# Transformer block on one core: the order of products, weight loads and stores in the feed-forward part

## Chip, core and metric

The kernel runs on one core of a Trainium2 chip, in one launch. The metric is device time in microseconds. TensorE is PE in the profile, VectorE DVE, ScalarE ACT, GpSimd POOL; SyncE (SP) issues nearly all the DMAs.

## What is computed

One layer for 2048 tokens of width 1024: a combined input projection, two kinds of attention, an output projection with residual, and a SwiGLU feed-forward part of width 2816. The change touches the last lines:

```python
h = h + jnp.einsum('bse,ed->bsd', mix, w_out[l])
u2 = rms_norm(h, norm2_w[l])
gate = jnp.einsum('bsd,df->bsf', u2, w_gate[l])
up = jnp.einsum('bsd,df->bsf', u2, w_up[l])
h = h + jnp.einsum('bsf,fd->bsd', jax.nn.silu(gate) * up, w_down[l])
```

## The kernel before

The feed-forward part runs over `steps`: two halves of 1024 tokens, and in each half 11 groups of 256 hidden columns. A step does `gate`, sometimes `down`, then `up`. Each matrix is cut into 2 x 2 blocks, and the 8 block products are replaced by 7 (combinations of blocks are formed first, and the results are added up in three running sums). Every number is kept as two f16 parts, high and low, so a block product is 12 matmuls of 512 columns (three part pairs by four slices of 128 rows), and `gate` or `up` is 7 products, 84 matmuls. `down` is 84 matmuls for each step whose activations it takes up, two steps at a time, so 168 in every second step.

`quad` writes the seven products in this order: `pa` (first part), two `pm`, `pa` again (accumulated on its first part), `pd`, `pm`, `pd` again. ACT copies `pa` at L1014 before it is accumulated on, and DVE reads `pd` at L1031 before its second part; L1035 and L1038 add the last two. `on_gate` applies silu on ACT (L1049), `on_up` multiplies on DVE (L1069) and forms the combinations of the activations.

The weights come in the first half through `load_ffn`, once for each of gate, up and down ("g", "u", "d") and step. A load takes one of two staging buffers (`stages`, filled by a DMA at L909 or L911), squares it on ACT into `sq`, of which there is one buffer (L937 for g and u, L189 for d), gets column maxima through PE into a PSUM tile `fsc` (8 matmuls at L945 for g and u, two small ones at L182 for d), makes a power-of-two scale in a chain of one-column DVE instructions (L175 to L204), and splits the blocks into high (ACT, L215) and low parts (DVE, L220). Four combinations are formed with `tt` on POOL (L98); three of them overwrite blocks of `stages`, one goes to `sx`. At the end the split weights are stored to `split` (L986), and the second half reads them back (L928).

`begin` runs a load up to the squares; `end` runs the rest. Both are called from hooks inside `gate`, `up` and `down`: the square of the next gate weights stands in the middle of `gate`, the rest of it at the start of `down`, and so on. In `up`, the down weights are ended and then the next up weights begun. `build_x` makes the last four token tiles of the second half's input in the background of the first two steps; `tick` advances it.

The program order is not the order on an engine: the framework places each instruction with a timeline of its own, and once placed, an engine takes its instructions strictly in that order. `tc.issue_after(x)` puts an edge into that plan: what is inside is placed behind x. PSUM has 8 tiles, taken in turn by `pst`.

Of the kernel before, what the change touches and what calls it, by code (L numbers as in the profile page):

```python
# [40 lines left out]
CU = 3  # L41
# [18 lines left out]
def block(tc, a, out):  # L60
# [3 lines left out]
    with top:  # L64
# [113 lines left out]

        def across(dst, pt, cols):
            k = len(cols)  # L180
            for j, c in enumerate(cols):
                PE.matmul(pt[:, P * j : P * j + P], lhsT=c.to_broadcast([P, P]), rhs=id32[:], start=True, stop=True)  # L182
            DVE.tensor_reduce(dst, pt[:, : P * k], op=ALU.max, axis=AX.X)
# [689 lines left out]
        with ExitStack() as ph2:  # L873
# [32 lines left out]

            def fetch(st, f0, nme):
# [12 lines left out]
            def load_ffn(half, fg, names, W):  # L920
                eng = "ADP" if fg == 0 else WE
                sc = scales.setdefault(fg, {})
                for nme in names:
                    if half == 1:
                        yield
                        late = nme == "d" and fg == NFG - 1
                        w16 = (fd if nme == "d" and not late else fw).tile([P, 7, 2, 512], F16, tag="wd" if nme == "d" and not late else "wgu", bufs=2, name=nm("w" + nme))
                        SP.dma_start(w16[:].rearrange("p o s n -> p (o s n)"), split[fg, "gud".index(nme)])  # L928
                        W[nme] = w16
                        continue  # L930
# [12 lines left out]
                    def columns(m):  # L943
                        for k in range(KT):
                            PE.matmul(pt[:, :256], lhsT=ones[:], rhs=sq[:, 256 * k : 256 * k + 256], start=k == 0, stop=k == KT - 1)  # L945
                        DVE.tensor_reduce(m, pt[:, :256], op=ALU.max, axis=AX.X)

                    scale_end((lambda m: across(m, pt, cols)) if nme == "d" else columns, r[:], p[:], True, sW)
                    sc[nme] = (r, p, sW)
                    sW = sc[nme][2]  # L950
                    tte = "DP" if fg == 0 else "P"
                    sx = fw.tile([P, 512], F32, tag="sx", bufs=1, name=nm("sx"))

                    def put(o, src, n):
                        split_weight(w16[:, o : o + n, 0], w16[:, o : o + n, 1], src, 512 * n, sW, eng)

                    if nme == "d":
                        sv = st.rearrange("p (f h n) -> p h f n", f=2, h=2)
                        b11, b21, b12, b22 = sv[:, 0, 0], sv[:, 0, 1], sv[:, 1, 0], sv[:, 1, 1]
                        put(0, sv[:, 0], 2)  # L960
                        tt(sx[:], b22, b12, ALU.subtract, 512, tte)
                        tt(b12, b12, b11, ALU.subtract, 512, tte)
                        tt(b11, b22, b12, ALU.subtract, 512, tte)
                        tt(b21, b21, b11, ALU.subtract, 512, tte)
                        put(2, sv[:, 1], 2)
                        put(4, sv[:, 0], 2)
                        put(6, sx[:].unsqueeze(1), 1)
                    else:
                        sv = st.rearrange("p (d k f n) -> p d k f n", d=2, k=4, f=2)
                        xv = sx[:].rearrange("p (k n) -> p k n", k=4)  # L970
                        wv = w16[:].rearrange("p o s (k n) -> p o s k n", k=4)

# [7 lines left out]
                        tt(blk(0, 0), blk(1, 0), blk(0, 0), ALU.subtract, 512, tte)  # L980
                        tt(blk(0, 1), blk(0, 1), blk(0, 0), ALU.subtract, 512, tte)
                        putk(2, sv[:, :, :, 1, :], 2)
                        putk(4, sv[:, :, :, 0, :], 2)
                        putk(6, xv.unsqueeze(1), 1)
                    W[nme] = w16
                    SP.dma_start(split[fg, "gud".index(nme)], w16[:].rearrange("p o s n -> p (o s n)"))  # L986
                if half == 0 and "g" in names:
# [12 lines left out]
            def product(ps_, wv, wo, X, xo, start, stop):  # L1000
                q = 0
                for kt in range(4):
                    for xi, wi in ((0, 0), (1, 0), (0, 1)):
                        PE.matmul(ps_[:].rearrange("p (t n) -> p t n", n=P), lhsT=wv[:, wo, wi, 128 * kt : 128 * kt + 128], rhs=X[xo][:, :, xi, kt, :], start=start and q == 0, stop=stop and q == 11, skip_group_check=not start)  # L1004
                        q += 1

            def quad(wv, X, tag, bufs, c11, hook=None):
                def cst():
# [7 lines left out]
                product(p6, wv, 4, X, 4, True, True)  # L1016
                DVE.tensor_tensor(u2[:], p6[:], u2[:], ALU.add)
                p7 = pst("pm")
# [12 lines left out]
                DVE.tensor_tensor(c22[:], pd[:], u3[:], ALU.add)  # L1031
                c11(1, 1, c22)
                p4 = pst("pm")
                product(p4, wv, 3, X, 6, True, True)
                DVE.tensor_tensor(u3[:], u3[:], p4[:], ALU.subtract)  # L1035
                c11(1, 0, u3)
                product(pd, wv, 5, X, 3, False, True)
                DVE.tensor_tensor(u2[:], u2[:], pd[:], ALU.add)  # L1038
                c11(0, 1, u2)

            def gate(W, X, hook=None):
                sg = {}
# [8 lines left out]

                quad(W["g"], X, "cg", 5, on_gate, hook)
                note("A", 2000)
                return sg

            def up(W, X, sg, hook=None, final=False):
                if final:
# [25 lines left out]

                quad(W["u"], X, "cu", CU, on_up, hook)
                note("D", 2440)
                return act

            def load_hs(half, j, final=False):
                if half == 1 and j % 2 and not final:
                    h = [stages[:, j // 2, D * q : D * q + D] for q in range(2)]  # L1090
# [6 lines left out]
            def down(half, units, hs, last, hook=None):  # L1097
# [3 lines left out]
                def prod(po, ao, wo, j, start=True):  # L1101
                    for u, (W, act) in enumerate(units):
                        for q, (xi, wi) in enumerate(((0, 0), (0, 1), (1, 0))):
                            PE.matmul(po[:], lhsT=act[:, ao, xi, 128 * j : 128 * j + 128], rhs=W["d"][:, wo, wi, :], start=start and u == 0 and q == 0, stop=u == nu - 1 and q == 2, skip_group_check=not start)  # L1104

# [12 lines left out]
                for j in range(4):  # L1118
                    if j == 2 and hook is not None:
                        hook()  # L1120
                    if j + 1 < 4:
                        hs.append(load_hs(half, j + 1, nu == 3))
                    h0, h1 = hs[j]
# [31 lines left out]
            def build_x():  # L1155
# [11 lines left out]
                for j in (2, 3):  # L1167
# [6 lines left out]
                    for z in (xa, xb):  # L1174
                        for h in range(2):
                            tr = pst("xtr")
                            for k in range(4):
                                PE.transpose(tr[:, P * k : P * k + P], z[:, 512 * h + P * k : 512 * h + P * k + P], id32[:])
                            ACT.copy(z[:, 512 * h : 512 * h + 512], tr[:])
# [40 lines left out]
            for i, (half, fg) in enumerate(steps):  # L1220
# [47 lines left out]
                if i == 0:  # L1268
                    tick(1)
                units.append((W, act))  # L1270
# [27 lines left out]
```

## Time and profile before

| | us |
|---|---|
| median of 3 runs (2700.67 to 2704.35) | 2701.52 |
| profiled execution, its own time | 2702.93 |
| its span | 2701.0 |
| feed-forward, first product starts at | 1425.19 |
| last `up` of the first half starts at | 2059.52 |

All stretches are in microseconds from the start of the span. A row of the timeline gives start, duration, engine, line, operation, tiles and how many were merged; in square brackets the idle time of the engine ahead of it and what ended that. Consecutive matmuls overlap, so the time that a product takes is read from start to start.

### The profile page before, as it was taken

How to read it: one execution, taken by the hardware profiler on the slowest of the kernel's cores; microseconds unless marked ns; L12 is line 12 of the kernel's file. 1: busy time of each engine (PE TensorE's matmuls, PEld its weight loads, DVE VectorE, ACT ScalarE, POOL GpSimd, SP SyncE). 2: the span in 40 equal slices, each digit the busy share in tenths (PEclk: the TensorE clock that was granted, in tenths of full speed). 3: DMA queues.
4: the chain of work that ended last, by engine and by line, in shares of the span. 5: the costliest groups of instructions: out<-in, count | busy, mean ns of one | idle time of the engine just before them, and what ended most of it. 6: DMA issues, size and time to landing. Idle time of an engine off the chain costs nothing. (4 is left out here: it accounts for less than half of the span.)

```text
span 2701.0 us, 50505 instructions
## 1 busy us (share of the span) xinstructions
PE 2508.6 (93%) x19628; PEld 1507.6 (56%) x19628; DVE 1959.8 (73%) x3712; ACT 1344.7 (50%) x2487; POOL 1517.8 (56%) x1097
## 2 busy tenths in 40 slices
PE   7998989899988989889999999999999999999999
PEld 4655656577776776567774444444444444444444
DVE  6898879899989889887866877778685543433434
ACT  4665656567978878765634534435352112111121
POOL 2578767768767767545665755665564332322323
PEclk9999999999999999999999999999999999999999
DMA  6778697768989989997996566565748744635532
GB/s 221 211 163 184 143 200 172 172 145 183 195 175 185 178 166 206 208 205 203 230 317 232 211 232 219 207 239 183 253 171 330 304 159 157 234 132 184 202 110 94
DMA packets 619584, 534.40 MB, mean 198 GB/s; under 512 B 480640, under 2 KB 548224, under 8 KB 609104
## 3 DMA queue, kind: packets, MB, share of 16 engines
q1 hardware_dynamic: 617520, 529.09, 70.1%
q8 instruction: 154, 2.52, 0.4%
q0 software_dynamic: 512, 1.36, 0.2%
q14 instruction: 86, 0.70, 0.1%
q10 hardware_dynamic: 1312, 0.72, 0.1%
HBM read 261.08 MB, written 147.32 MB: 151 GB/s over the span
## 5 line engine op out<-in xcount | busy, mean ns | idle before, releaser
L98 POOL TENSOR_TENSOR s<-z,s 128x1024 f16<-128x1024 f32 (+7 forms) x288 | 471.5, 1646 | 141.8 <-ACT s L89 118.2
L506 PE MATMUL sc<-kT,qT 128*128 128x512 f16 (+3 forms) x1520 | 382.7, 354 | 51.1 <-DVE z L622 18.6
L1104 PE MATMUL pd<-wd,act 128*128 128x512 f16 x1764 | 392.8, 380 | 5.3 <-DVE cu L1038 4.7
L621 DVE TENSOR_TENSOR_SCAN z<-z,sc 128x512 f32<-128x512 f32 (+3 forms) x320 | 352.8, 1112 | 56.5 <-ACT sc L619 34.6
L325 PE MATMUL pj<-w,xt 128*128 128x384 f16 x1920 | 354.6, 333 | 17.1 <-ACT raw L374 5.8
L1004 PEld LDWEIGHTS <-wu 128*128 128x128 f16 x1848 | 181.9, 98 | 224.6 <-issue 12.8
L1004 PEld LDWEIGHTS <-wg 128*128 128x128 f16 x1848 | 181.3, 98 | 222.9 <-issue 9.3
L517 PE MATMUL yp<-v,aT 128*128 128x64 f16 (+1 forms) x4896 | 271.2, 205 | 36.9 <-DMA aT<-s 35.7
L517 PEld LDWEIGHTS <-aT 128*128 128x128 f16 x4896 | 239.1, 100 | 114.4 <-DMA aT<-s 46.7
L98 POOL TENSOR_TENSOR act<-cg,act 128x512 f16<-128x512 f32 x109 | 150.7, 1393 | 259.4 <-ACT act L1063 259.4
L1104 PEld LDWEIGHTS <-act 128*128 128x128 f16 x1764 | 172.9, 98 | 213.5 <-issue 7.2
L325 PEld LDWEIGHTS <-xt 128*128 128x128 f16 x1920 | 187.8, 99 | 147.2 <-issue 23.4
L89 ACT CAST s<-z 128x128 f16<-128x128 f32 (+7 forms) x215 | 173.3, 810 | 135.9 <-DMA aT<-s 44.6
L98 POOL TENSOR_TENSOR stages<-stages 128x512 f32<-128x512 f32 x97 | 171.4, 1767 | 116.5 <-DVE wg L220 42.2
L618 ACT ACTIVATE z<-sc,c 128x512 f32<-128x512 f32 (+3 forms) x320 | 211.2, 665 | 24.4 <-PE sc L506 12.4
L98 POOL TENSOR_TENSOR hs<-hs,cu 128x512 f32<-128x512 f32 x102 | 133.6, 1317 | 159.3 <-DVE hs L1110 59.7
L506 PEld LDWEIGHTS <-qT 128*128 128x128 f16 x1520 | 128.8, 99 | 119.7 <-issue 23.9
L831 PE MATMUL po<-wo,mt 128*128 128x256 f16 x1536 | 182.4, 279 | 12.6 <-DVE xf L834 8.6
L1063 ACT CAST act<-cg 128x512 f16<-128x512 f32 x126 | 76.7, 616 | 231.1 <-DVE cg L1069 192.7
L1110 DVE SCALAR_TENSOR_TENSOR hs<-pd,c,hs 128x512 f32<-128x512 f32 x144 | 106.0, 747 | 115.0 <-PE pd L1104 105.3
L341 PE MATMUL pj<-xt,w 128*128 128x128 f16 x2304 | 177.4, 222 | 6.2 <-DVE v L363 5.2
L1004 PE MATMUL pm<-X,wu 128*128 128x512 f16 x792 | 179.8, 381 | 2.1 <-ACT cg L1049 1.7
(254 smaller groups left out, 4812.3 us busy)
## 6 DMA issues: line engine op xcount, KB each, us to landing
xt<-xs SPq DMA_DIRECT2D x112, 512.0 KB, 4.5
hs<-hd SPq DMA_DIRECT2D x72, 512.0 KB, 4.5
hd<-hs SPq DMA_DIRECT2D x56, 512.0 KB, 5.9
split<-wg SPq DMA_DIRECT2D x11, 1792.0 KB, 6.9
split<-wu SPq DMA_DIRECT2D x11, 1792.0 KB, 6.7
split<-wd SPq DMA_DIRECT2D x11, 1792.0 KB, 6.8
wg<-split SPq DMA_DIRECT2D x11, 1792.0 KB, 7.5
wd<-split SPq DMA_DIRECT2D x11, 1792.0 KB, 9.0
```

What stands on the lines that cost most here:

```text
L89: ACT.copy(dst, src)
L98: (DVE if e == "D" else POOL).tensor_tensor(dst, a_, b_, op)
L325: PE.matmul(pj[:, :384], lhsT=xv[:, xi, kt, :], rhs=G["w"][:, wi, kt, :], start=n == 0, stop=n == 23)
L341: PE.matmul(o, lhsT=x_ if c == 2 else w_, rhs=w_ if c == 2 else x_, start=n == 0, stop=n == 23)
L506: last = PE.matmul(sc[:, : 128 * w].rearrange("p (t n) -> p t n", n=P), lhsT=G["q"][i // 4][:, a_, i % 4, :], rhs=G["k"][q][:, b_, 0:w, :] ...
L517: PE.matmul(yp[:, y0 : y0 + wd], lhsT=aT[:, a_, :], rhs=v[:, v_ : v_ + wd], start=start and j == 0 and q == 0, stop=stop and j == nb - 1 a ...
L618: ACT.activation(om[:, lo:hi], sc[:, :w], AF.Sigmoid, scale=G["nkz"][:])
L621: DVE.tensor_tensor_scan(ov, ov, sc[:, :w], om[:, hi : hi + 1], op0=ALU.mult, op1=ALU.bypass)
L831: PE.matmul(po[:, sl], lhsT=mt[:, kt, P * xi : P * xi + P], rhs=wos[2 * h + n][wi][:, kt, :], start=q == 0, stop=q == 23)
L1004: PE.matmul(ps_[:].rearrange("p (t n) -> p t n", n=P), lhsT=wv[:, wo, wi, 128 * kt : 128 * kt + 128], rhs=X[xo][:, :, xi, kt, :], start=st ...
L1104: PE.matmul(po[:], lhsT=act[:, ao, xi, 128 * j : 128 * j + 128], rhs=W["d"][:, wo, wi, :], start=start and u == 0 and q == 0, stop=u == nu ...
L1110: DVE.scalar_tensor_tensor(dst, po[:], kd[:], src, op0=ALU.mult, op1=ALU.add)
```

## The change

Seven edits, all in the feed-forward part. (1) In `quad`, `pd` stands ahead of the second part of `pa`, so that two products lie between the two parts of `pa` beyond the first two, and two between the parts of `pd`. (2) `front` remembers the last product written; the matmuls of the column maxima and the transposes of `build_x` get an edge behind it. (3) `build_x` advances one step at each of several hooks, in the first two steps. (4) In `up`, the next up weights are begun before the down weights are ended. (5) The two last combinations of a load go to `sq`, seen as f32 (`mix`), and no longer to `stages`. (6) The stores to `split` are queued behind the next loads. (7) In the last `down` of the first half, every second pair of residual rows comes into `stages`, as it did before in the second half.

```diff
-        def across(dst, pt, cols):
+        def across(dst, pt, cols, where=None):
+            with where or nullcontext():
...
+            front = [None]
+
+            def behind():
+                return tc.issue_after(front[0]) if front[0] is not None else nullcontext()
...
                     fetch(st, f0, nme)
+                store(1)
                 return st
+
+            unsaved = []
+
+            def store(n):
+                while len(unsaved) > n:
+                    dst, w16 = unsaved.pop(0)
+                    SP.dma_start(dst, w16[:].rearrange("p o s n -> p (o s n)"))
...
                     if half == 1:
+                        store(0)
                         yield
...
                     def columns(m):
-                        for k in range(KT):
-                            PE.matmul(pt[:, :256], lhsT=ones[:], ...)
+                        with behind():
+                            for k in range(KT):
+                                PE.matmul(pt[:, :256], lhsT=ones[:], ...)
...
+                    mix = sq[:].bitcast(F32).rearrange("p (d n) -> p d n", d=2)
...
-                        tt(b11, b22, b12, ALU.subtract, 512, tte)
-                        tt(b21, b21, b11, ALU.subtract, 512, tte)
+                        tt(mix[:, 0], b22, b12, ALU.subtract, 512, tte)
+                        tt(mix[:, 1], b21, mix[:, 0], ALU.subtract, 512, tte)
                         put(2, sv[:, 1], 2)
-                        put(4, sv[:, 0], 2)
+                        put(4, mix, 2)
...
-                    SP.dma_start(split[fg, "gud".index(nme)], w16[:].rearrange("p o s n -> p (o s n)"))
+                    unsaved.append((split[fg, "gud".index(nme)], w16))
...
-                product(pa, wv, 1, X, 1, False, True)
-                c11(0, 0, pa)
-                note("D", 3000)
-                note("A", 500)
-                if hook is not None:
-                    hook()
                 pd = pst("pd")
                 product(pd, wv, 2, X, 2, True, True)
...
                 c11(1, 1, c22)
+                product(pa, wv, 1, X, 1, False, True)
+                c11(0, 0, pa)
+                note("D", 3000)
+                note("A", 500)
+                at(5)
                 p4 = pst("pm")
...
-                if half == 1 and j % 2 and not final:
+                if (half == 1 or last) and j % 2 and not final:
...
                 def in_up():
+                    begin("u", *steps[i + 1], "u", Wn) if more else None
                     end("d")
-                    if i == 0:
-                        tick(3)
-                    begin("u", *steps[i + 1], "u", Wn) if more else None
-
-                sg = gate(W, X, in_gate)
-                if i < 2:
-                    tick(3 if i == 0 else 16)
+                    one()
+
+                def one():
+                    if i < 2:
+                        tick(1)
+
+                sg = gate(W, X, {2: one, 5: in_gate} if i == 1 else {5: in_gate})
...
-                act = up(W, X, sg, in_up, not more)
+                act = up(W, X, sg, {2: one, 3: one, 5: in_up, 6: one}, not more)
                 end("u")
-                if i == 0:
-                    tick(1)
+                if i < 2:
+                    tick(16 * i + 1)
```

Lines of the changed kernel are higher by 1 (L182 to L183) up to 24 (L1104 to L1128); L937, L945, L986 and L1004 became L952, L961, L919 and L1022.

The first place is ACT, in an `up` that follows a `down` in the middle of the first half. `sq` are squares (3530 of the down weights, 3562 or 3559 of the next up weights), `wd` the down weights' high parts, `act` the activations' high parts. Before:

```order
L937 ACTIVATE sq3562_25542<-stages_21846 128x2048
L1014 COPY cu3550_25464<-pa3549_25451 128x512
L1063 CAST act3548_25450<-cg3495_25099 128x512
L215 ACTIVATE wd3554_25510<-stages_21846,c3529_25320 128x2x512 x2
L215 ACTIVATE wd3554_25510<-sx3557_25520,c3529_25320 128x512
L1063 CAST act3548_25450<-cg3501_25120 128x512
L215 ACTIVATE wd3554_25510<-stages_21846,c3529_25320 128x2x512
```

The same place now:

```order
L1036 COPY cu3550_25463<-pa3549_25450 128x512
L1087 CAST act3548_25449<-cg3496_25097 128x512
L1087 CAST act3548_25449<-cg3497_25112 128x512
L216 ACTIVATE wd3560_25533<-stages_21846,c3529_25319 128x2x512 x2
L216 ACTIVATE wd3560_25533<-sq3530_25320,c3529_25319 128x2x512
L216 ACTIVATE wd3560_25533<-sx3563_25543,c3529_25319 128x512
L1087 CAST act3548_25449<-cg3494_25082 128x512
L952 ACTIVATE sq3559_25531<-stages_21846 128x2048
```

The squares of the up weights stood ahead of the down weights' splits and stand behind them now, since the splits read the one buffer `sq`.

The second place is PE in the same `up`, the first row of each product alone: `fsc` by `id` is the down weights' maxima, `fsc` by `ones` the up weights', `wu` products are the `up`, `wg` products the next `gate`. Before:

```order
L182 MATMUL fsc3555_25511<-id32_63,m03531_25322 128x128
...
L1004 MATMUL pd3563_25544<-X3103_22147,wu3484_25008 128x512
...
L1004 MATMUL pm3565_25562<-X3104_22149,wu3484_25008 128x512
...
L945 MATMUL fsc3568_25607<-sq3562_25542,ones_21847 128x256
...
L1004 MATMUL pa3571_25637<-X3085_21890,wg3521_25282 128x512
```

The same place now:

```order
L183 MATMUL fsc3561_25534<-id32_63,m03531_25321 128x128
...
L1022 MATMUL pm3565_25560<-X3104_22147,wu3484_25006 128x512
...
L1022 MATMUL pd3554_25494<-X3112_22366,wu3484_25006 128x512
...
L1022 MATMUL pm3574_25663<-X3087_21893,wg3521_25281 128x512
...
L961 MATMUL fsc3568_25605<-sq3559_25531,ones_21847 128x256
...
L1022 MATMUL pa3571_25634<-X3085_21889,wg3521_25281 128x512
```

Between the two maxima there were two products and are now three, the last of them from the next `gate`.

The third place is SP's queue behind that `up`, where three loads follow each other. Before:

```order
L986 DMA split_85<-wd3554_25510 128x7168
L911 DMA stages_21846<-in_w_gate_dram 128x8x256
L986 DMA split_85<-wu3567_25606 128x7168
L909 DMA stages_21846<-in_w_down_dram 128x2x1024
L986 DMA split_85<-wg3584_25746 128x7168
```

Now:

```order
L925 DMA stages_21846<-in_w_gate_dram 128x8x256
L919 DMA split_85<-wd3560_25533 128x7168
L923 DMA stages_21846<-in_w_down_dram 128x2x1024
L919 DMA split_85<-wu3567_25604 128x7168
L925 DMA stages_21846<-in_w_up_dram 128x8x256
```

Each load stood right behind a store and stands ahead of it now.

More of the change, by code (lines that the diff above doesn't have):

```diff
@@ L943, in columns @@
                     def columns(m):
-                        for k in range(KT):
-                            PE.matmul(pt[:, :256], lhsT=ones[:], rhs=sq[:, 256 * k : 256 * k + 256], start=k == 0, stop=k == KT - 1)
+                        with behind():
+                            for k in range(KT):
+                                PE.matmul(pt[:, :256], lhsT=ones[:], rhs=sq[:, 256 * k : 256 * k + 256], start=k == 0, stop=k == KT - 1)
                         DVE.tensor_reduce(m, pt[:, :256], op=ALU.max, axis=AX.X)
-                    scale_end((lambda m: across(m, pt, cols)) if nme == "d" else columns, r[:], p[:], True, sW)
+                    scale_end((lambda m: across(m, pt, cols, behind())) if nme == "d" else columns, r[:], p[:], True, sW)
                     sc[nme] = (r, p, sW)
@@ L1103, in prod @@
                         for q, (xi, wi) in enumerate(((0, 0), (0, 1), (1, 0))):
-                            PE.matmul(po[:], lhsT=act[:, ao, xi, 128 * j : 128 * j + 128], rhs=W["d"][:, wo, wi, :], start=start and u == 0 and q == 0, stop=u == nu - 1 and q == 2, skip_group_check=not start)
+                            front[0] = PE.matmul(po[:], lhsT=act[:, ao, xi, 128 * j : 128 * j + 128], rhs=W["d"][:, wo, wi, :], start=start and u == 0 and q == 0, stop=u == nu - 1 and q == 2, skip_group_check=not start).ins
                 def ust():
@@ L1121, in down @@
                     if j + 1 < 4:
-                        hs.append(load_hs(half, j + 1, nu == 3))
+                        hs.append(load_hs(half, j + 1, nu == 3, last))
                     h0, h1 = hs[j]
@@ L1176, in build_x @@
                             tr = pst("xtr")
-                            for k in range(4):
-                                PE.transpose(tr[:, P * k : P * k + P], z[:, 512 * h + P * k : 512 * h + P * k + P], id32[:])
+                            with behind():
+                                for k in range(4):
+                                    PE.transpose(tr[:, P * k : P * k + P], z[:, 512 * h + P * k : 512 * h + P * k + P], id32[:])
                             ACT.copy(z[:, 512 * h : 512 * h + 512], tr[:])
```

33 lines of the change are left out of this document (20 added, 13 removed).

## The prediction

> **What bounds the kernel now.** The page gives the engines, and the windows then show where PE is full and where not.
>
> ```profile
> span 2701.0 us, 50505 instructions
> PE 2508.6 (93%) x19628; PEld 1507.6 (56%) x19628; DVE 1959.8 (73%) x3712; ACT 1344.7 (50%) x2487; POOL 1517.8 (56%) x1097
> 1680.01:1800.14 120.13, 115.16 (x542) 0.99 0.60 210
> 1800.14:1921.34 121.20, 116.41 (x543) 0.97 0.63 219
> 2191.00:2299.91 108.91, 108.91 (x506) 1.00 0.50 179
> ```
>
> A window's columns are its length, PE's busy time with its matmuls, the granted clock, the DMA share and GB/s. Each of the first two is a pair of steps of the first half, the third a pair of the second half, where weights are only read back: there PE is busy all the time at full clock, and no order can take anything from it. What can be won lies in the first half. Its size comes from the timeline of PE.
>
> ```profile
> 1425.19 2.75 PE L1004 MATMUL pa<-X,wg 128*128 128x512 f16 x12
> 1679.13 1.04 PE L945 MATMUL fsc<-sq,ones 128*128 128x256 bf16 x8
> 1680.01 18.29 PE L1104 MATMUL pd<-wd,act 128*128 128x512 f16 x84
> 1698.14 2.11 PE L1004 MATMUL pa<-X,wu 128*128 128x512 f16 x9
> 1709.79 0.39 PE L182 MATMUL fsc<-id,m 128*128 128x128 f32 x2
> 1710.01 2.75 PE L1004 MATMUL pd<-X,wu 128*128 128x512 f16 x12
> 2059.52 2.54 PE L1004 MATMUL pa<-X,wu 128*128 128x512 f16 x11
> ```
>
> From start to start, 84 matmuls take 1698.14 - 1680.01 = 18.13 us (0.2158 each, 2.59 for a block product of 12), the column maxima of a gate or up load 0.88, those of a down load 0.22. A pair of steps holds 504 matmuls, four of the first kind of maxima and two of the second: 108.8 + 3.5 + 0.4 = 112.7 us. The two pairs are 7.4 and 8.5 us longer, 7.9 in the mean. From 1425.19 to 2059.52, 634.3 us, stand 31 times 84 matmuls less 6 that come later (2598: 560.7 us), 20 and 10 maxima (17.6 and 2.2) and the 32 transposes of L1178, 7.1 us by a row below: 587.6. So 46.7 us is all that the change can win. The waits of PE in this stretch (total, times, longest) say for what:
>
> ```profile
> PE fsc L182 <- ACT sq L189: 6.3, 3, 2.3
> PE fsc L945 <- ACT sq L937: 5.9, 4, 2.0
> PE pd L1104 <- DVE cu L1038: 4.7, 2, 2.8
> PE pd L1004 <- DVE cg L1031: 3.6, 4, 1.6
> PE xtr L1178 <- DVE bx L228: 3.4, 2, 3.1
> PE xtr L1178 <- DVE xrs L155: 2.8, 1, 2.8
> PE pa L1004 <- ACT cu L1014: 2.0, 1, 2.0
> PE pa L1004 <- ACT cg L1014: 1.7, 1, 1.7
> PE pm L1004 <- ACT cg L1049: 1.7, 1, 1.7
> ```
>
> These nine make 32.1 us. Much of the rest is clock that falls behind a gap:
>
> ```profile
> 1751.87 0.49 PE L182 MATMUL fsc<-id,m 128*128 128x128 f32 x2 [2.28 <-ACT sq L189]
> 1752.20 4.44 PE L1004 MATMUL pd<-X,wu 128*128 128x512 f16 x12
> 1783.95 2.75 PE L1004 MATMUL pd<-X,wg 128*128 128x512 f16 x12 [1.62 <-DVE cg L1031]
> 1750.00:1758.00 8.00, 6.13 (x22) 0.79 0.36 143
> ```
>
> After a gap of 2.28 us the next twelve matmuls took 4.44 us instead of 2.75, at a granted clock of 0.79: 1.7 us more. After 1.62 us they took 2.75. I charge 1.7 to a gap above 2 us and nothing to one below 1.7. [...]
>
> **The change part by part.** *Products two apart (1).* The second part of `pa` waited for L1014's copy (2.0, 1.7), that of `pd` for L1031 (3.6 in four waits), since one product or none stood between. Two products, 5.2 us, cover a copy and an addition of under 1 us with what is queued ahead of them. I take these 7.3 us as won; if DVE is behind by over 5 us, as it was where PE waited 2.8 for L1038, up to that much stays.
>
> *Stores behind loads (6).* SP's queue and ACT at one down load:
>
> ```profile
> 1740.36 0.32 SPq L986 DMA_DIRECT2D split<-wu  x1
> 1740.79 0.38 SPq L909 DMA_DIRECT2D stages<-in_w_down_dram  x1
> 1749.82 1.91 ACT L189 ACTIVATE sq<-stages 128x2048 bf16<-128x2048 f32 x1 [3.66 <-DMA stages<-in_w_down_dram]
> ```
>
> A store of 1.8 MB leaves 0.43 us ahead of the load, and the load lands 9 us after its issue; Square then starts late by 3.66 us and PE by 2.28. With the order turned the load has the DMA engines to itself first. The 6.3 us of L182 and most of the 5.9 of L945 have this cause. What is queued behind the load is then the store, for which nothing in this half waits but the buffer of its own weights, two loads later.
>
> *Combinations in the squares' buffer (5), up load ahead of down scale (4).* In before, POOL overwrote a block of `stages` only when the low part of it was done; now it writes to `sq` and needn't wait for that. In return `sq` isn't free until the split of `mix` has been read, so the next load's Square waits for the end of this load's split. The rows for that chain:
>
> ```profile
> 1711.92 2.19 ACT L215 ACTIVATE wd<-stages,c 128x1024 f16<-128x1024 f32 x2 [0.52 <-DVE c L204]
> 1766.14 2.22 DVE L220 SCALAR_TENSOR_TENSOR wd<-stages,c,wd 128x1024 f16<-128x1024 f32 x1 [1.22 <-ACT wd L215]
> L220 DVE SCALAR_TENSOR_TENSOR wd<-stages,c,wd x18: 1271/1748/2296, 1592.1 to 1889.7; 128x1024 f16<-128x1024 f32 x18
> L220 DVE SCALAR_TENSOR_TENSOR wd<-stages,c,wd 128x1024 f16<-128x1024 f32 x30 | 50.7, 1703 | 5.8 <-ACT wd L215 5.8
> L98 POOL TENSOR_TENSOR stages<-stages 128x512 f32<-128x512 f32 x87 | 153.9, 1769 | 105.6 <-DVE wg L220 38.4 <-DVE wd L220 31.1 <-DVE wu L220 25.3
> L1035 DVE TENSOR_TENSOR cu<-cu,pm 128x512 f32<-128x512 f32 x10 | 6.8, 677 | 0.0
> L1069 DVE SCALAR_TENSOR_TENSOR cg<-pa,c,cg 128x512 f32<-128x512 f32 x10 | 7.4, 744 | 6.8 <-PE pa L1004 6.8
> L1178 PE MATMUL xtr<-id,bx 128*128 128x128 f32 x32 | 7.1, 387 | 6.2 <-DVE bx L228 3.4 <-DVE xrs L155 2.8
> ```
>
> POOL idled 105.6 us for the low parts; before, the last of them ended 1768.36 - 1752.20 = 16.2 us behind the end T of the down maxima. Now the chain from T is: first high part at 1711.92 - 1710.18 = 1.74; the product that runs meanwhile ends at T + 2.59; then DVE has its addition (0.68), a low part (1.28, near the shortest of 18), a multiplication (0.75), a low part, an addition (0.68), the low part of `mix`: T + 8.54. Square of the up load takes 1.91 more, T + 10.45. With the mean low part of 1.70 it is T + 11.7.
>
> PE reaches the up maxima after 36 matmuls (7.77 us) or 41 (8.85) in one kind of pair, and after 60 or 69 (12.9 or 14.9) in the other. So it stalls 2.7 to 3.9 (middle 3.3) and 1.6 to 2.9 (2.2) in the one, with 1.7 of clock each: 8.9. In the other the up maxima stall nothing; a down maximum stands 48 matmuls (10.36 us) behind the gate's, against the same chain: 0.7. Mean 4.8 a pair. I add 1.5 for waits that I can't name (PE's for L1049 and L1038 have 1.7 to 2.8 each and no edit of theirs): 6.3 against 7.9, 1.6 won. From about 1560 on, 499.5 us, there are 4.15 pairs: 6.6 us.
>
> *Edges and single steps (2, 3).* 46.7 - 4.15 x 7.9 = 13.9 us of the excess lie in the first pair. The two waits of the transposes are 6.2 of these, and two gaps near 3 us cost 3.4 of clock: 9.6. Advanced one step at a time, a row's normalization lies several products ahead of its transposes. I take four fifths, 7.7, since rows that are read behind a store could land late.
>
> *Residual rows in `stages` (7).* Two loads more stand ahead of the input's loads at the half's end, and the last store behind them: 0 to 1 us, taken as 0, hidden by the last `down` and `up` of the half; without that cover, the time of 1 MB, some 5 us at the 210 GB/s of the window.
>
> Sum: 7.7 + 6.6 = 14.3 us. The profiled execution's own time is 2702.9, the median of the runs 1.4 lower: 2701.5 - 14.3 = 2687.
>
> **The rivals.** *The squares' buffer is the bound (slower).* In a step without `down` three loads pass through one `sq` one after the other, while PE needs 168 x 0.2158 + 1.76 + 0.22 = 38.2 us. One load holds it for Square (1.91), half a product until PE takes the maxima (1.3), these (0.88), and the chain (8.54): 12.6 us. With mean low parts 13.9; with two combinations of 1.77 on POOL in the chain instead of beside it, 17.4. The rate decides from (38.2 + 7.9) / 3 = 15.4 us on. At 17.4 a pair has 52.2 - 38.2 = 14.0 of excess, 6.1 more than now: 25.3 in all, less the 7.7 of the start, 2719; at 16.5 it is 2708. For it: DVE and POOL are busy 73% and 56%, and the low parts are 1.27 us at the shortest and 1.75 at the median of 18, which looks like blocking. Against it: POOL now begins ahead of the scale, and a step with `down` has 36 us more to catch up. [...]
>
> *Each wait is replaced.* The order is fixed ahead, with no slack where it puts a reader: take one cause away and the next instruction on DVE is late (L1038, L1049). Only part of the start is won, or nothing: 2694 to 2704. For it: nine causes share 32 us, none over 6.3. Against: two of them are gone by distance.
>
> *The edges remove nearly all of it.* No stall in either kind of pair, and the mean low part short: the excess per pair falls to 2 and at the start to 4: 2701.5 - 24.5 - 9.9 = 2667, with 2660 to 2676 around it.
>
> **How the numbers follow.** Forecast, 2677 to 2694: 0.55. Squares' buffer, 2700 to 2725: 0.20, of it 0.02 within 0.2% (5.4 us, about what a measurement of this kernel can tell from no change). Replaced waits: 0.15, of it 0.10 within 0.2%. All removed: 0.10. So faster 0.55 + 0.10 + 0.05 = 0.70, same 0.12, slower 0.18. The range 2668 to 2708 leaves out half of the third rival (0.05) and the worse half of the first (0.10).
>
> **What would show it.** Right: in PE's waits the rows for copies, L1031's successor and the transposes are gone, and those for Square at the up maxima are there, 2 to 4 us each in every second pair; Square waits for DVE's last low part and no longer for a DMA. Pairs take 118 to 120 us. Wrong: pairs above 122 with Square waiting for DVE at all three loads of a step without `down` (first rival); pairs of 120 to 121 with waits under other names (second); pairs under 116 (third). A window of the second half away from 108.9 would mean that something else has moved.

## The result and the profile after

The changed kernel takes 2687.93 us (median of 4 runs, 2686.33 to 2694.22) against 2701.52 before. The ratio of the runs is 0.9956, with a 95% interval of 0.9941 to 0.9971 (the two medians alone give 0.9950). The forecast was 2687. The profiled execution is the longest of the four; its page begins:

```profile
span 2692.0 us, 50574 instructions
PE 2500.0 (93%) x19628; PEld 1504.3 (56%) x19628; DVE 1935.1 (72%) x3710; ACT 1345.5 (50%) x2487; POOL 1481.5 (55%) x1099
```

VectorE and GpSimd are busy 25 and 36 us less with nearly the same number of instructions, so these have become shorter in the mean. In this execution the first gate product starts at 1429.88, before at 1425.19. The work ahead of it is untouched but for its last instructions; in fourteen profiles of this kernel, the one before and their variants this start lies anywhere from 1419.91 to 1429.88. So below a kernel is also judged by the *stretch* from its first gate product to the end of the span: 1275.8 us before, 1262.1 here, and 1264.0 in another execution of the same kernel. These two differ by 1.8 us, so a difference of 2 us is taken to mean nothing. Each of the other kernels has one profile, and how far its stretch varies isn't known.

The windows of PE show where the stretch became shorter. First before, the start, one pair and the last piece of the first half (two more pairs stand in the prediction):

```profile
1425.19:1556.53 131.34, 120.19 (x576) 0.97 0.59 212
1556.53:1680.01 123.48, 115.32 (x543) 0.99 0.65 226
1921.34:2059.52 138.18, 132.56 (x618) 0.99 0.63 222
```

The same five pieces after:

```profile
1429.88:1557.88 128.00, 119.19 (x574) 0.96 0.62 224
1557.88:1681.61 123.73, 116.72 (x543) 0.97 0.58 211
1681.61:1796.61 115.00, 113.03 (x542) 1.00 0.62 227
1796.61:1918.22 121.61, 115.04 (x542) 0.99 0.57 210
1918.22:2051.15 132.93, 130.29 (x618) 1.00 0.63 228
```

The pieces are 3.3, -0.3, 5.1, -0.4 and 5.3 us shorter: 13.1 together. What follows them, nearly all of it the second half, takes 640.9 us against 641.5. Of the pairs every second one becomes shorter, by 5 us, and the others don't. The waits of PE in this part, after:

```profile
PE pd L1022 <- DVE cg L1049: 7.5, 3, 7.1
PE fsc L961 <- ACT sq L952: 5.8, 2, 3.1
PE pd L1128 <- DVE hs L1134: 4.4, 2, 2.2
PE pm L1022 <- ACT cg L1073: 4.1, 2, 2.4
PE pd L1128 <- ACT cu L1154: 3.9, 3, 1.6
```

The waits for ScalarE's copies of `pa`, for the transposes and at the down maxima are gone; those for Square at the up maxima have become two long ones, one in each pair that isn't shorter. The rows of one of them:

```profile
1590.26 0.38 PE L183 MATMUL fsc<-id,m 128*128 128x128 f32 x2
1597.65 1.89 DVE L221 SCALAR_TENSOR_TENSOR wd<-sq,c,wd 128x1024 f16<-128x1024 f32 x1
1599.57 1.91 ACT L952 ACTIVATE sq<-stages 128x2048 bf16<-128x2048 f32 x1 [2.35 <-DVE wd L221]
1601.53 1.53 PE L961 MATMUL fsc<-sq,ones 128*128 128x256 bf16 x8 [3.12 <-ACT sq L952]
```

The down maxima end at T = 1590.64, the low part of the combinations at T + 8.9, Square of the up weights at T + 10.8. PE has come after 36 matmuls and waits 3.1 us. This is the chain of the prediction (T + 8.54, T + 10.45, a stall of 2.7 to 3.9).

### The profile page after: what moved, and what is told of

The parts are those of the page before. It is cut to its first block, busy times and chain, and to the rows that moved or that the text cites. A ratio compares the mean times of both kernels' runs of the same rounds, so it can differ in the third digit from the quotient of the medians.

```text
span 2692.0 us, 50574 instructions
## 1 busy us (share of the span) xinstructions
PE 2500.0 (93%) x19628; PEld 1504.3 (56%) x19628; DVE 1935.1 (72%) x3710; ACT 1345.5 (50%) x2487; POOL 1481.5 (55%) x1099
## 4 chain that ended last, share of the span: by engine, by line
PE 41%; DVE 5%; POOL 2%; issue 2%; ACT 1%; DMA 0%; SPq 0%; POOLq 0%; DVEq 0%; ACTq 0%
PE pd L1128 14%; PE pm L1022 10%; PE pa L1022 7%; PE pd L1022 7%; DVE wd L221 1%; PE po L832 1%; PE fsc L961 1%; DVE cg L98 0%; DVE cg L1093 0%; DVE wu L221 0%; POOL z L98 0%; DVE wg L221 0%; POOL sx L98 0%; POOL b L98 0%; POOL sq L98 0%
## 5 line engine op out<-in xcount | busy, mean ns | idle before, releaser
L1128 PE MATMUL pd<-wd,act 128*128 128x512 f16 x1764 | 391.9, 379 | 8.5 <-DVE hs L1134 4.4
L1022 PEld LDWEIGHTS <-wg 128*128 128x128 f16 x1848 | 182.3, 99 | 229.6 <-issue 16.2
L1022 PEld LDWEIGHTS <-wu 128*128 128x128 f16 x1848 | 181.0, 98 | 218.2 <-issue 3.5
L1128 PEld LDWEIGHTS <-act 128*128 128x128 f16 x1764 | 172.4, 98 | 217.2 <-issue 10.5
L832 PE MATMUL po<-wo,mt 128*128 128x256 f16 x1536 | 181.9, 278 | 14.3 <-DVE xf L835 8.8
L1022 PE MATMUL pm<-X,wu 128*128 128x512 f16 x792 | 179.1, 379 | 4.1 <-ACT cg L1073 4.1
L1134 DVE SCALAR_TENSOR_TENSOR hs<-pd,c,hs 128x512 f32<-128x512 f32 x136 | 100.6, 747 | 113.7 <-PE pd L1128 113.5
L1022 PE MATMUL pm<-X,wg 128*128 128x512 f16 x792 | 179.1, 379 | 0.0
```

The lines of the kernel that those rows point to most:

```text
L832: PE.matmul(po[:, sl], lhsT=mt[:, kt, P * xi : P * xi + P], rhs=wos[2 * h + n][wi][:, kt, :], start=q == 0, stop=q == 23)
L1022: front[0] = PE.matmul(ps_[:].rearrange("p (t n) -> p t n", n=P), lhsT=wv[:, wo, wi, 128 * kt : 128 * kt + 128], rhs=X[xo][:, :, xi, kt, : ...
L1128: front[0] = PE.matmul(po[:], lhsT=act[:, ao, xi, 128 * j : 128 * j + 128], rhs=W["d"][:, wo, wi, :], start=start and u == 0 and q == 0, s ...
L1134: DVE.scalar_tensor_tensor(dst, po[:], kd[:], src, op0=ALU.mult, op1=ALU.add)
```

## The experiments

All were timed in five rounds beside the kernel before. "Stretch" is of one profile each.

| kernel | ratio to before (95%) | stretch, us |
|---|---|---|
| all seven edits, once more | 0.9957 (0.9941 to 0.9973) | 1264.0 |
| without (6) | 0.9957 (0.9942 to 0.9972) | 1262.1 |
| without (5) | 1.0117 (1.0099 to 1.0135) | 1304.4 |
| without (5) for the down weights | 0.9985 (0.9969 to 1.0001) | 1271.2 |
| without (1) | 0.9970 (0.9957 to 0.9984) | 1268.3 |
| without (2) | 0.9942 (0.9921 to 0.9962) | 1256.9 |
| (5) alone | 0.9988 (0.9975 to 1.0001) | 1274.2 |
| (5) and (1) alone | 0.9988 (0.9976 to 1.0001) | 1272.4 |
| (6) alone | 1.0080 (1.0056 to 1.0103) | 1302.9 |
| all, input's low parts on GpSimd | 0.9960 (0.9945 to 0.9975) | 1263.5 |
| all, up load ended in the next gate | 0.9882 (0.9861 to 0.9902) | 1243.8 |
| the same, without (2) | 0.9899 (0.9881 to 0.9917) | 1245.8 |

**All edits once more.** No edit. (The 124.2 us in the expectation's second sentence is a slip and enters nothing.)

> The changed kernel once more, as the base for the next ones. Its first profile had 124.2 us less to tell apart than its time says: that run took 2694.22 us where the other three took 2686.33 to 2688.58, and its feed-forward part began 4.7 us later than before. Theory: those 4.7 us lie ahead of every edit and vary from run to run; the feed-forward part up to the last up of the first half takes 621 us as in the first profile (634.3 before), and the time is 2686 to 2689. Rival: the edits delay the work ahead of the first gate product (the down maxima stand there now); then it starts near 1430 again whenever the time is above 2690, and near 1430 in this profile too.

The median was 2689.99 (12 runs); the feed-forward part began at 1420.04, and the start of it took 127.1 us, not 128.0. The rival wanted a start near 1430 in this profile too, and falls: the 4.7 us at the front vary from run to run, as the first theory has it, though the median is 1 us above its range.

**Stores ahead of loads.**

```diff
-                    unsaved.append((split[fg, "gud".index(nme)], w16))
+                    SP.dma_start(split[fg, "gud".index(nme)], w16[:].rearrange("p o s n -> p (o s n)"))
```

> Edit (6) undone alone: each store is queued where its split ends, ahead of the next load. Theory A (the prediction's step): the loads land late again, ScalarE's Square waits for their DMA, and PE pays some 2 us with clock at two or three maxima of the steady pairs: 2693 to 2698. Theory B: with the combinations in the squares' buffer Square waits for VectorE's last low part, and the loads are issued and landed several us ahead of it (a load issued at 1737.00 in the trace, its Square at 1751.35), so the order of loads and stores no longer matters: 2686 to 2690, with no wait of Square for a DMA above 1 us.

2689.81 us, as with the edit. But this was no test of a turned queue: the order of all five queues came out exactly as with edit (6). With the combinations in `sq` the staging buffer is free before their low part is taken, and the plan puts the next load ahead of the store by itself. The kernel without the up load begun ahead of the down scale (4), which was not timed, gets the same order on all five queues too. So in this kernel each of (4) and (6) does nothing, and 1262.1 is a third stretch of one and the same order.

**Combinations back in the staging buffer.** Edit (5) undone:

```diff
-                        tt(mix[:, 0], b22, b12, ALU.subtract, 512, tte)
-                        tt(mix[:, 1], b21, mix[:, 0], ALU.subtract, 512, tte)
+                        tt(b11, b22, b12, ALU.subtract, 512, tte)
+                        tt(b21, b21, b11, ALU.subtract, 512, tte)
...
-                        put(4, mix, 2)
+                        put(4, sv[:, 0], 2)
```

and the same for gate and up.

> Edit (5) undone alone: the two last combinations go to the staging buffer again. Theory A: GpSimd waits again for the first low part before it overwrites a block (88 us in the steady part before), the low parts last 1.5 to 1.8 us in the mean instead of 1.3, the splits end late; the pairs in which nothing stalls now (115.0 us) go back to 117 to 120: 2692 to 2699. Theory B: the buffer of the squares is only a cost (PE's 3.1 and 2.7 us for Square at the up maxima), and without it the pairs that stall (123.7 and 121.6) lose 3 to 5 us each: 2678 to 2684.

2732.11 us, 30 slower than before and 42 slower than with the edit: beyond the first theory's price, and the second theory falls. Rows of one place, in order of start, show how lateness reaches PE:

```profile
1766.18 1.29 DVE L221 SCALAR_TENSOR_TENSOR wg<-stages,c,wg 128x1024 f16<-128x1024 f32 x1 [0.95 <-ACT wg L216]
1774.04 1.91 ACT L952 ACTIVATE sq<-stages 128x2048 bf16<-128x2048 f32 x1 [4.25 <-DMA stages<-in_w_up_dram]
1776.36 2.18 ACT L216 ACTIVATE wd<-stages,c 128x1024 f16<-128x1024 f32 x2
1777.54 2.48 DVE L221 SCALAR_TENSOR_TENSOR wd<-stages,c,wd 128x1024 f16<-128x1024 f32 x2 [4.83 <-ACT wd L216]
1797.16 3.15 PE L1022 MATMUL pd<-X,wg 128*128 128x512 f16 x7 [5.45 <-DVE cg L1049]
```

The load of the up weights is issued at 1767.49, when the last low part of the gate weights has read the staging buffer. Square waits 4.25 us for it, the down weights' high parts stand behind Square on ScalarE, and VectorE waits 4.83 us for these. From there VectorE has work without a gap up to the addition that PE waits for (5.45 us). GpSimd's wait for the first low part (1.28 us) and ScalarE's for GpSimd (4.28 us), with the activations' copies queued behind, are there too, but VectorE doesn't stand still for them at this place. So here it is the buffer that comes free late.

**The same for the down weights alone.** The three changed lines above, without those for gate and up.

> The changed kernel with edit (5) undone for the down weights only: their combinations go to the staging buffer, those of gate and up stay in the squares' buffer. The square of the up weights then needn't wait for the down split. Theory A: PE's waits of 3.1 and 2.7 us for Square at the up maxima, with 1 to 2 us of clock, go, and GpSimd's wait for the down weights' low parts comes back where nobody waits: the stretch from the first gate product is 1256 to 1261. Theory B: what hurts without edit (5) is the in-order queue, splits that wait for GpSimd with the activations' copies behind them on ScalarE; with a third of that back, the stretch grows by a third of 41, to 1270 to 1280.

1271.2: the second theory. The waits at the up maxima do go (0.6 us are left), as the first theory said, but PE's waits for the addition of `pd` at L1049 grow from 7.5 to 25.4 us.

**Edit (5) alone; (5) and (1); (6) alone.** Each is made in the kernel before. For (5) it is the diff of the combinations read the other way, for (1) that of the run after these, also read the other way; for (6):

```diff
                     fetch(st, f0, nme)
+                store(1)
                 return st
...
-                    SP.dma_start(split[fg, "gud".index(nme)], w16[:].rearrange("p o s n -> p (o s n)"))
+                    unsaved.append((split[fg, "gud".index(nme)], w16))
```

> The kernel before with edit (5) alone: the two last combinations go to the squares' buffer. Undone alone it cost 41 us of the stretch from the first gate product to the end (1262 to 1264 us with all edits, 1275.8 before, 1304.4 with all but this one). Theory A: it is the main edit by itself; GpSimd's wait for low parts goes, the steady pairs fall from 120 to 121 us to 116 to 118, the stretch takes 1262 to 1268 and the kernel 2689 to 2695. Theory B: it pays only with the products two apart, since one buffer makes the loads serial and the maxima come up too early in the old order; the stretch takes 1272 to 1285 and the kernel 2698 to 2712.

> The kernel before with edits (5) and (1) alone: combinations in the squares' buffer and products two apart, without edges, single steps, turned stores and residual rows in the staging buffer. Measured so far, from the first gate product to the end: 1275.8 before, 1274.2 with (5) alone, 1268.3 with all but (1), 1262 to 1264 with all. Theory A: (5) and (1) together make the steady pairs (115.0 and 121 to 124 us) and so most of the gain; the stretch takes 1264 to 1268, and what is left, 2 to 5 us, is the start with its transposes. Theory B: edges and single steps matter as much, and the stretch takes 1269 to 1274.

> The kernel before with edit (6) alone: stores queued behind the next loads. Theory A (the prediction's step): PE's waits at the down maxima (6.3 us) and most of those at the others (5.9), which end with late loads, go, with their clock: the stretch from the first gate product falls from 1275.8 to 1264 to 1270, the kernel to 2690 to 2697. Theory B: the load goes ahead of the store, but the staging buffer comes free only behind the low parts; the stretch stays within 3 us of 1275.8, or grows as it does with all edits but (5), where it is 1304.

(5) alone hardly moves the stretch (1274.2, the second theory's side). With (1) it is 1272.4, again the second theory's side. But the windows show the first theory right on the pairs; the start and three pairs:

```profile
1426.65:1563.84 137.19, 124.01 (x575) 0.94 0.57 209
1563.84:1684.25 120.41, 115.04 (x543) 0.99 0.59 219
1684.25:1800.82 116.57, 114.56 (x543) 0.99 0.60 221
1800.82:1920.87 120.05, 115.20 (x543) 0.99 0.58 215
```

The three pairs take 357.0 us, with all edits 360.3, before 364.8. So (5) and (1) make all that the steady pairs win; the start is 9 us longer than with all edits. What shortens it again must lie in (2), (3) or (7), since (4) and (6) change no order on any queue in this kernel either. (7) acts at the half's end only, and (2) is not it (the run without edges, below). That leaves the single steps (3), by elimination; no run has them alone.

(6) alone is 27 us longer, not 6 to 12 shorter: the second theory, in its worse case. The loads come ahead of the stores, and PE's waits behind VectorE grow all the same. Waits of PE, then of GpSimd, in that kernel:

```profile
PE pd L1013 <- DVE cg L1040: 16.9, 6, 4.5
PE pa L1013 <- ACT cg L1023: 10.2, 3, 4.5
POOL stages L98 <- DVE wg L220: 49.2, 8, 10.2
```

Before, GpSimd's wait of the last row was 37.3 us. A possible reason is that the plan spaces the steps of a load by its own times, in which the store's transfer counts: with the load earlier it would draw the splits together, and GpSimd, waiting for low parts, couldn't follow. No run shows this; the cause of the 27 us stays open.

**Second part of pa early.**

```diff
+                product(pa, wv, 1, X, 1, False, True)
+                c11(0, 0, pa)
+                note("D", 3000)
+                note("A", 500)
                 pd = pst("pd")
...
-                product(pa, wv, 1, X, 1, False, True)
-                c11(0, 0, pa)
-                note("D", 3000)
-                note("A", 500)
```

> Edit (1) undone alone: the second part of pa stands ahead of pd again, one product behind the two pm. Theory A: PE's waits for the copy of pa and for the addition behind pd come back, 7.3 us in the first half of the profile before, of these 3.6 at pd: 2691 to 2695. Theory B: these waits only stood where VectorE and ScalarE were late for another cause, which is gone: 2686 to 2689.

2693.89 us, stretch 1268.3: the first theory's amount, but not its cause. PE's wait for the copy is 1.1 us in all; what grows is another row:

```profile
PE fsc L961 <- ACT sq L952: 12.3, 4, 4.2
```

That was 5.8 in two waits. In this order the plan has the up maxima 36 matmuls behind the down maxima at both places of the stalling pairs, where the changed kernel has 36 and 41. It isn't the whole account: the waits in the `down` fall from 8.3 to 2.4 us, and all of PE's waits in the first half grow from 26.7 to 30.7.

**No edges.**

```diff
-                return tc.issue_after(front[0]) if front[0] is not None else nullcontext()
+                return nullcontext()
```

> Edit (2) undone alone: no edge holds the column maxima and the transposes behind the last product written. Theory A: the steady pairs stay as they are, since the plan has the maxima at the same products there; in the first two steps maxima and transposes come ahead of their inputs again and PE waits 2 to 6 us more: the stretch from the first gate product 1264 to 1270. Theory B: the edges hold back more than they save, and the stretch falls to 1258 to 1262.

The second theory, 1 us below its range: 2685.59 us, stretch 1256.9. The start takes 126.2 us and a stalling pair 120.4 instead of 123.7. By the stretch the edges cost 5 to 7 us here, though the intervals of the two ratios overlap.

**Low parts of the input on GpSimd.**

```diff
-                    yield from x_ops([d2(z) for z in (xa, xb)], d2(xt), 1, j, bufs, "AP", "DP")
+                    yield from x_ops([d2(z) for z in (xa, xb)], d2(xt), 1, j, bufs, "AP", "P")
```

> The changed kernel with one more change: the low parts of the second half's input that build_x forms (128x1024 subtractions, 1.2 to 2.3 us each on VectorE) go to GpSimd alone. In the trace after, PE waits 7.1 us for the addition of pd at the gate of the second step, and twelve matmuls behind it take 5.28 us instead of 2.75. Theory A: VectorE was behind there by its own work, the input's part of it 4 to 6 us; without it the wait shrinks to under 3 us and the stretch from 1262 to 1264 to 1254 to 1259. Theory B: the late rows' loads and GpSimd's square root hold VectorE, not its load; the stretch stays above 1260.

This was to take away the long wait in the second step. Rows of VectorE there in the changed kernel, and PE's:

```profile
1487.65 0.69 DVE L1044 TENSOR_TENSOR cg<-pm,cg 128x512 f32<-128x512 f32 x1
1488.26 1.30 DVE L229 SCALAR_TENSOR_TENSOR bx<-bx,xrs,bx 128x1024 f32<-128x1024 f32 x1
1489.48 1.27 DVE L221 SCALAR_TENSOR_TENSOR wu<-stages,c,wu 128x1024 f16<-128x1024 f32 x1
1490.68 1.27 DVE L229 SCALAR_TENSOR_TENSOR bx<-bx,xrs,bx 128x1024 f32<-128x1024 f32 x1
1491.87 1.27 DVE L221 SCALAR_TENSOR_TENSOR wu<-stages,c,wu 128x1024 f16<-128x1024 f32 x1
1493.07 0.68 DVE L1049 TENSOR_TENSOR cg<-pd,cg 128x512 f32<-128x512 f32 x1
1493.80 5.28 PE L1022 MATMUL pd<-X,wg 128*128 128x512 f16 x12 [7.08 <-DVE cg L1049]
```

Four long instructions stand ahead of the addition of `pd`, and none is a low part of the input: two normalize its rows (L229), two are low parts of the up weights. With the input's low parts elsewhere PE still waits 6.0 us there, and the stretch is 1263.5: the second theory's time. The wait is now put down to L155, a small step ahead of the rows' normalization that ends just after the addition (1489.1), so the addition is late there too, behind four low parts of the up weights. Which part the rows' loads and GpSimd's root have in it isn't shown.

**The up load ended in the next gate.** In the first half `end("u")` no longer follows `up`:

```diff
+            late_u = [lambda: None]
...
+                def fin_u(f=late_u[0]):
+                    f()
+                    if i == 1:
+                        one()
...
-                sg = gate(W, X, {2: one, 5: in_gate} if i == 1 else {5: in_gate})
+                sg = gate(W, X, {2: fin_u, 5: in_gate})
...
-                end("u")
+                late_u[0] = lambda n=nxt: [None for _ in n.pop("u", ())]
+                if not more or half == 1:
+                    end("u")
```

> The changed kernel with one more change: in the first half the up weights' load is ended in the next gate, behind its second pm, and no longer at the end of up. PE then comes to the up maxima 67 or 68 matmuls behind the down maxima, where it came after 36, 41 or 60. Theory A (the prediction's chain): Square of the up weights ends 10.5 to 11.7 us behind the down maxima, 36 matmuls take 7.8 and 68 take 14.7, so the waits of 3.1 and 2.7 us with their clock go; the gate's maxima, 52 matmuls (11.2 us) later, wait under 1 us; pairs that stall fall from 121 to 124 to 116 to 119, and the stretch from 1262 to 1264 to 1252 to 1258. Theory B: three loads through one buffer are the bound in a step without down, so what is won at the up maxima is lost at the gate's and the down's: 1260 to 1268.

2668.98 us (6 runs), 0.9882 of before: the first theory, and 8 to 14 us better than it said. It is the fastest kernel here. The start and three pairs, the up maxima with their Square, and the one long wait that is left:

```profile
1423.61:1553.20 129.59, 117.74 (x574) 0.97 0.63 233
1553.20:1666.63 113.43, 112.87 (x542) 1.00 0.61 226
1666.63:1781.03 114.40, 113.06 (x542) 1.00 0.60 225
1781.03:1893.75 112.72, 112.72 (x543) 1.00 0.62 228
1595.11 1.91 ACT L952 ACTIVATE sq<-stages 128x2048 bf16<-128x2048 f32 x1 [0.76 <-DVE wd L221]
1600.47 1.04 PE L961 MATMUL fsc<-sq,ones 128*128 128x256 bf16 x8
...
1489.04 4.04 PE L1022 MATMUL pd<-X,wg 128*128 128x512 f16 x12 [8.46 <-DVE cg L1049]
```

Square still ends 11.1 us behind the down maxima (T = 1585.96), but PE comes 14.5 us behind them and waits for nothing. One pair takes 112.72 us, which is the sum of its matmuls alone, so three loads through one `sq` in a step without `down` are not a bound. The theory counted the two stalls alone. With the maxima the whole end of the load has moved, the splits too, and PE's other waits in the first half, for L1134, L1154 and L1073, have fallen from 12.4 to 1.3 us.

**The same without the edges.**

> The up weights' load ended in the next gate as in the last run, and edit (2), the edges, left out. From the first gate product to the end that run took 1243.8 us, and one wait of 8.5 us is left in it, at the gate of the second step, where VectorE has two normalized rows and three low parts ahead of the addition of pd that PE waits for, with twelve matmuls slowed behind it. Without the edges the plan puts that addition ahead of the rows and low parts. Theory A: the wait shrinks to the 3.5 us that it has with the edges alone left out, and the two gains add up: the stretch takes 1235 to 1240, the kernel 2660 to 2666. Theory B: the work on VectorE only moves behind and is waited for a product later, at the transposes: 1241 to 1246, the kernel as in the last run.

2671.41 us (5 runs): the second theory in kind. The wait of 8.5 us at the second step's gate shrinks, and another comes behind it:

```profile
1483.03 5.28 PE L1022 MATMUL pd<-X,wg 128*128 128x512 f16 x12 [3.81 <-DVE cg L1049]
1491.77 4.44 PE L1022 MATMUL pm<-X,wu 128*128 128x512 f16 x12 [2.76 <-DVE cg L1058]
```

Two buffers for the squares, and a start with other single steps, weren't tried.

## Why the prediction was right, and where it was not

The time came out at 2687.9 against 2687. By the ratio the gain is 12 us, 8 to 16, against 14.3. That it is so near is in part luck: two terms were off in opposite ways, by 3.1 and 4.4 us, and one step had the wrong mechanism. The main path was right: one buffer, whose chain holds PE at every second pair.

*The stalling pairs* were forecast at 112.7 + 8.9 + 1.5 = 123.1 us and took 123.7 and 121.6; the others at 112.7 + 0.7 + 1.5 = 114.9 and took 115.0. The stall behind 36 matmuls was 3.1 and 2.7 us, forecast 2.7 to 3.9. The one behind 41 isn't there: PE waits 1.55 and 2.2 us ahead of it, in the `down`, for L1154 and L1134, waits with the size of the allowance for the unnamed. Over all pairs 9.7 us were won; the forecast had 6.6. It took the mean of two pairs before, 120.6 us, for all of them, but the two that stall now took 123.5 and 121.2 before, so they lost 0.3 and 0.4 us and not 2.5 each.

*The start* was to give 7.7 and gave 3.3 in this profile and 4.2 in the other. The transposes' two waits did go, as forecast. What the step missed is the wait of 7.1 us on VectorE's addition of `pd` with 2.5 us of slower matmuls behind. It is the successor of L1031, whose row was to be gone: the second rival's mechanism, in one place. And the edges, which the step counted with the single steps as a gain, are a loss of 5 to 7 us in this kernel (in the last two runs, 1243.8 and 1245.8, they make no difference that can be told).

*Stores behind loads* was wrong as a mechanism. It credited the waits at the down maxima (6.3) and most of those at the others to the order in SP's queue. The waits went, but that order follows from edit (5) without edit (6), and (6) on its own costs 27 us. The share of ScalarE's waits makes the real step plain, before and then after, from 1560 to the half's end:

```profile
ACT sq L937 <- DMA stages<-in_w_up_dram: 59.2, 6, 14.2
ACT sq L189 <- DMA stages<-in_w_down_dram: 23.6, 5, 8.6
...
ACT sq L190 <- DVE wg L221: 19.1, 8, 3.0
ACT sq L952 <- DVE wu L221: 13.8, 4, 4.3
ACT sq L952 <- DVE wd L221: 13.1, 7, 2.4
```

Square waited for transfers, and waits for low parts now: the buffer comes free earlier, so the load is issued earlier (at one down load 14.4 us ahead of its Square, 9.0 before). With (5) undone and (6) kept Square waits for transfers again, 67.3 us from 1560 to 2050, and 42 us are lost. The sum was not hurt, since it only needed these waits to go.

*Products two apart* was booked at 7.3 us for the waits on the copy and the addition. Undone, it cost 4 to 6 us, mostly by way of the up maxima and not by these waits.

*The first rival* (squares' buffer as the bound) had the right wait at the wrong rate: the chain is real and holds PE at one place, but the last run but one shows three loads in a step fitting into the matmuls' own time.

## What to carry to other kernels

When one edit frees a buffer earlier, the order that another edit was written to enforce may follow by itself: compare the order on the queues with and without each edit before crediting it. Where a chain through one buffer has a length that can be added up from the profile (here 11 us), place its reader on the critical engine beyond that length: ending the load later, with its reader 67 instead of 36 matmuls behind the chain's start, won 18 to 20 us, more than all seven edits. Edits that help together can hurt alone, so undoing one and doing one alone are different questions.

## What was not expected of the hardware

The same kind of instruction changed its length from one kernel to the other. A low part of the up weights, 128x512 from `sx`, on VectorE, had a mean of 1756 ns in the steady part before and has 740 now; those from `stages` for the down weights fell from 1766 to 1296, and those from `sq` are 1805:

```profile
L220 DVE SCALAR_TENSOR_TENSOR wu<-sx,c,wu 128x512 f16<-128x512 f32 x8 | 14.0, 1756 | 0.0
L221 DVE SCALAR_TENSOR_TENSOR wu<-sx,c,wu 128x512 f16<-128x512 f32 x8 | 5.9, 740 | 0.0
L221 DVE SCALAR_TENSOR_TENSOR wd<-sq,c,wd 128x1024 f16<-128x1024 f32 x8 | 14.4, 1805 | 0.0
```

What ran on GpSimd at the time went with the length. From 1560 to 2050 in the two traces, the 55 low parts of 128x1024 with less than 0.15 us of a GpSimd instruction beside them took 1269 to 1286 ns, the 22 of 128x512 took 735 to 746 (all of these in the changed kernel), and each of the 84 longer ones (up to 2360) had GpSimd beside it. GpSimd alone doesn't make one long: 31 short ones had it beside them too. What sets the long ones apart from these 31 isn't shown.

A gap of the same length at the same place cost 1.7 us in one kernel and nothing in another. The changed kernel, then the one without edges:

```profile
1975.02 2.75 PE L1022 MATMUL pm<-X,wu 128*128 128x512 f16 x12 [2.44 <-ACT cg L1073]
1962.29 4.44 PE L1022 MATMUL pm<-X,wu 128*128 128x512 f16 x12 [2.44 <-ACT cg L1073]
```

So the prediction's rule, 1.7 us for every gap above 2 us, is no rule: behind 2.44 us the twelve matmuls took 2.75 us in the changed kernel, at a granted clock of 1.00 from 1975 to 1978, and 4.44 in the one without edges. What decides between the two isn't shown.
